# A two-layer decoder step: spilled gates and sums fetched ahead, a round's branch product in two halves around its transposes, and one weight split a step later

## The chip, the cores and the metric

The kernel runs on one core of a Trainium2 chip. TensorE (PE, with its weight loads PEld) multiplies, VectorE (DVE), ScalarE (ACT) and GpSimd (POOL) do the rest, and SyncE (SP) only issues transfers. The metric is the device time of one execution in microseconds (us); lower is better.

## The reference

One inference step of a decoder with two layers, for a prompt of 256 tokens and 64 sample tokens, which the kernel handles as one block of T = 320 columns. What matters here is how a layer ends:

```python
def _layer(x, ...):                       # prompt group: 256 tokens; sample group: 8 x 8 tokens with 2048 cached keys each
    xn = _rmsnorm(x, norm_g)
    h = xn @ w_in                         # one projection: pool, MLA and DeltaNet inputs, z gates, 3 x 1024 branch gates
    y_a = pool_mixer(h_pool) * silu(z_pool)
    y_b = mla(h_q, h_kv, h_kr, cached latents) * silu(z_mla)
    y_c = _rmsnorm(gated_delta(conv(h_qkv), beta, alpha)) * silu(z_dn)
    gates = sigmoid(h_gate)               # (tokens, 3, 1024)
    merged = (gates[:, :, 0] * (y_a @ w_br_pool) + gates[:, :, 1] * (y_b @ w_br_mla)
              + gates[:, :, 2] * (y_c @ w_br_dn))
    return x + merged @ w_out, caches and states
# two layers, then a final RMSNorm
```

## The kernel before

Activations lie transposed, 128 channels on the partitions and 320 tokens along the free dimension. A fp32 product is made of three fp32r products: a weight tile `wraw` comes from DRAM on SP's queue (four buffers), ACT rounds it into a high part `wh` (L200), DVE subtracts to get the low part `wl` (L201), and `mm3` (L224 to L226) issues for each 128-row block k the three matmuls wh by high, wh by low, wl by high. A buffer of `wraw` is free again when its `wl` is made.

Each layer goes through these stages:

1. Projections and DeltaNet. Of the branch gates, those of the DeltaNet branch (n = 1) and of the attention branch (n = 2) are computed along the way, 16 tiles of 128 x 320 (160 KB) a layer, and **spilled** to DRAM (`spilled[n, m]`, m being one of 8 slices of 128 output channels).
2. Prompt attention, one head a step (h = 0 to 10, a software pipeline): PE makes scores `hsc`; DVE takes maxima; ACT takes the exponential (`pS`); DVE takes a reciprocal and POOL scales (`head_scale`); PE transposes (`pT`), ACT copies (`pPT`), PE multiplies by the values (`po`). Two gates are computed in these steps; at h = 5 the weights of the second are split.
3. Eight **rounds**, one for each sample sequence bb. In a round PE makes the pool branch's gate product for slice m = bb (`gate`), a small product `olat` for the round before, eight transposes of the softmaxed scores `S` (`PT`) and one of the own keys (`PTn`), the pool branch's product `br` with w_br_pool (12 matmuls), the attention product `pv`, and the scores `sc` of the next sequence. DVE transposes the next sequence's keys (`flip`); POOL issues the gathers of later keys. At the end DVE forms (gate + 1) times `br` and ACT's queue stores it to DRAM as `sums[m]` (`first_sum`). All of these take banks from one PSUM pool "A" with four banks.
4. The **tail**: 16 branch products, n = 1 and 2 for m = 0 to 7; each goes into a bank, and `branch_out(n, m, b)` fetches the gate tile `gt` on POOL's queue (NG = 6 buffers), for the first product of a slice also `accs[m]` from `sums[m]` (four buffers `acc`), multiplies on DVE (L1360) and adds on POOL (L1361). The finished slice is halved and split by ACT and DVE into `mgH`, `mgL`, and eight products with w_out (24 matmuls each, tile `wo`) follow; each is added to the residual `xT`, which POOL's queue brings back from DRAM (1280 KB) near the start of the tail.

In stages 2 and 3 and at the start of the tail the order of PE, DVE, ACT and POOL is the order in which the code is written; after it a scheduler orders the instructions. Each engine executes in order: an instruction that waits holds up all behind it, and a transfer is issued only when the issuing engine comes to it. The lines around the transposes in a round:

```python
PT = turned_p(S)
PTn = turned_own(bb)
b = branch_mm(0, w0, "A")
weigh(bb, mx)
```

Of the kernel before, what the change touches and what calls it, by code (L numbers as in the profile page):

```python
# [11 lines left out]
F32 = mybir.dt.float32  # L12
# [19 lines left out]
KVB = 3  # L32
WSP = 2
THB = 2
NG = 6
ORD0 = (4, 5)
PRM, RNB, STB, XT, WLP = "M", "M", "M", ("A", "B"), 2
WARM, WN, TA = 8, 6, 1
# [78 lines left out]
def trunk(tc, I, O, layers=2):  # L117
    nc = tc.nc
# [24 lines left out]
    def ps(tag, name):  # L143
        return (banks.get(tag) or banks["pool"]).tile([128, 512], F32, tag=tag, name=name, bufs=banks["n"][tag])
# [269 lines left out]
    for l in range(layers):  # L414
# [931 lines left out]
            wname = branches[n][1]  # L1346
            return split_w(load_w(I[wname][l][:, m * 128 : m * 128 + 128], 4, 128)[:, :4, :], 4)

        def branch_mm(n, w, tag):
            b = ps(tag, "br")  # L1350
            mm3(b[:, :T], w, yb[branches[n][2]], 4)
            return b

        def branch_out(n, m, b):
            t = per.tile([128, T], F32, tag="gt", name="gt", bufs=NG)
            nc.gpsimd.dma_start(t, spilled[n, m])
            if m not in accs:
                accs[m] = p3a.tile([128, T], F32, tag="acc", name="acc", bufs=4)
                nc.gpsimd.dma_start(accs[m], sums[m])
            stt(t, t, 1.0, b[:, :T], add, mult)  # L1360
            nc.gpsimd.tensor_tensor(accs[m], accs[m], t, add)  # L1361

# [9 lines left out]
        with tc.manual_schedule(engines={mybir.EngineType.PE, mybir.EngineType.DVE, mybir.EngineType.Activation, mybir.EngineType.Pool}):  # L1372
# [23 lines left out]
            for h in range(11):  # L1396
                if h < 8:
                    hsc = hp_.tile([128, 512], F32, tag="H", name="hsc", bufs=4)
                    head_scores(h, hsc)
                    st2 = head_max(hsc)  # L1400
                    hs[h] = head_soften(hsc, st2), st2
                if h < 2:
                    values(h)
                if h == 4:
                    gather(1)
                if h == 5:
                    nm, w = gate_w()
                if h in flips:
                    flip(0, keys, flips[h])
                if h - 2 in hs:  # L1410
                    hp[h - 2] = head_turned(hs[h - 2][0])
                if h in (2, 3):
                    b = gate_mm("A", w, b, (4 * (h - 2), 4 * (h - 2) + 4))
                if h in (7, 8):
                    b = gate_mm("A", w, b, (4 * (h - 7), 4 * (h - 7) + 4))
                if h in hs:
                    head_scale(*hs[h])
                if h - 3 in hs:
                    head_attend(h - 3, hp[h - 3])
                if h == 3:  # L1420
                    gate_out(nm, b)
                    b = None
                if h == 8:
                    gate_out(nm, b)
                    pair[0] = paired[0] = 1
                    gs = gate_w(nm=(0, 0)), branch_w(0, 0)
                if h == 9:
                    hpc.close()
                    sp = bank4(spc, "sp")
                    sc = scores(keys, q4)  # L1430
# [6 lines left out]
            for bb in range(NB):  # L1437
                more = bb + 1 < NB
                if not more:

                    pdc.close()
                    p3a = p3e.enter_context(tc.tile_pool(name=f"p3a_{l}", bufs=1, reuse_waits="tile"))
                S = soften(bb, sc, mx)
                if more:
                    keys = key_tiles()
                    flip(bb + 1, keys, 0)
                    nmx = stats(bb + 1)
                softened(bb, S, mx)
                if more:
                    flip(bb + 1, keys, 1)  # L1450
                (nm, w), w0 = gs
                g = gate_mm("A", w)
                if o is not None:
                    ob = combine(o)
                    combined(bb - 1, ob)
                t = gate_out(nm, g)
                if more:
                    flip(bb + 1, keys, 4)
                    flip(bb + 1, keys, 2)
                PT = turned_p(S)  # L1460
                PTn = turned_own(bb)
                b = branch_mm(0, w0, "A")
                weigh(bb, mx)
                if not more:
                    w10 = branch_w(1, 0)
                    split_y(p3a, 8)
                    w11 = branch_w(1, 1)
                o = attend(bb, PT, PTn, mx)
                first_sum(bb, t, b)
                if more:  # L1470
                    flip(bb + 1, keys, 3)
                    gs = gate_w(nm=(0, bb + 1)), branch_w(0, bb + 1)
                    sc = scores(keys, q4)
                    mx = nmx
                    if bb + 2 < NB:
                        q4 = load_q(bb + 2)
# [23 lines left out]
            last = l == layers - 1  # L1500
            p3c, p3 = enter(f"p3_{l}", dict(pj=2, Y=2) if last else dict(pj=4))
            wcfg.update(pool=p3, n=2)
            w13 = branch_w(1, 3)
            split_y(p3, 4)
            w20 = branch_w(2, 0)
# [12 lines left out]
        for mp in range(4):  # L1518
# [3 lines left out]
                        branch(n, m, "A")  # L1522
            for m in (2 * mp, 2 * mp + 1):
                split_x(mg[0][:, m, :], mg[1][:, m, :], accs[m], scale=0.5)
        nm = Norm(p3)
        if last:

# [71 lines left out]
```

## Time and profile before

| | |
|---|---|
| Time, median of 3 runs | 1073.99 us (1073.39 to 1076.58) |
| The profiled execution's own time | 1067.52 us |
| Its span, first to last instruction | 1065.8 us |
| PE busy | 984.4 us (92%) |
| DVE busy | 692.1 us (65%) |
| ACT busy | 474.8 us (45%) |
| POOL busy | 279.2 us (26%) |
| Mean granted TensorE clock | 0.979 of full speed |

Busy time is the time in which an engine had an instruction under way; matmuls overlap, so their durations sum to more than the time they take. The profiled execution is 0.6% below the median of the other three. In a timeline the column after the start is the time from the start of the first to the end of the last of the instructions merged in the row, and the bracket gives the idle time of the engine before it and what ended it. Rows of `DMA_DIRECT2D` or `DMA_INDIRECT` on an engine are the issuing of a transfer, not its landing.

### The profile page before, as it was taken

The page shows a single profiled execution, that of the slowest core. Times are in us where ns is not written, and L with a number is a line of the kernel's source. Part 1 is how long each engine was busy: PE and PEld are TensorE (multiplying, and loading weights), DVE is VectorE, ACT ScalarE, POOL GpSimd, SP SyncE. Part 2 cuts the span into 40 slices and gives each one's busy share as a digit, 9 for nine tenths or more (in the row PEclk, how much of TensorE's full clock was granted, in tenths as well). Part 3 has the DMA queues.
Part 4 walks back from the last instruction along what each step waited for, and adds up shares of the span by engine and source line. Part 5 has one row for each costly group of instructions (what it writes and reads, how often), then busy time and mean ns, then how long its engine had stood idle before and what let it go on. Part 6 is the DMA issues. An engine that isn't in the chain of part 4 may idle for free. (4 is left out here: it accounts for less than half of the span.)

```text
span 1065.8 us, 24832 instructions
## 1 busy us (share of the span) xinstructions
PE 984.4 (92%) x10211; PEld 858.9 (81%) x10211; DVE 692.1 (65%) x1364; ACT 474.8 (45%) x878; POOL 279.2 (26%) x412
## 2 busy tenths in 40 slices
PE   8998999989999999978999999997999999999686
PEld 7897988978877877868888889896878777778686
DVE  4879857557546756555668997744565666575462
ACT  6664353364353323333567544426426433234243
POOL 1224113124242111036313432221241410102441
PEclk9999999999999999999999999998999999999898
DMA  8644444633564676368564454453356366644651
GB/s 231 185 132 112 120 114 109 168 86 97 156 217 149 202 247 224 104 194 248 142 182 130 115 139 112 110 149 84 95 146 193 136 212 218 234 156 149 206 172 50
DMA packets 206538, 165.78 MB, mean 156 GB/s; under 512 B 28344, under 2 KB 195026, under 8 KB 203850
## 3 DMA queue, kind: packets, MB, share of 16 engines
q1 hardware_dynamic: 176364, 98.47, 34.2%
q0 software_dynamic: 8384, 52.03, 13.8%
q10 hardware_dynamic: 21678, 13.71, 4.2%
q8 instruction: 80, 1.31, 0.5%
q14 instruction: 32, 0.26, 0.1%
HBM read 147.45 MB, written 16.96 MB: 154 GB/s over the span
## 5 line engine op out<-in xcount | busy, mean ns | idle before, releaser
L201 DVE TENSOR_TENSOR wl<-wraw,wh 128x1024 fp32r<-128x1024 f32 (+1 forms) x180 | 195.6, 1099 | 116.1 <-ACT wh L200 115.8
L200 ACT ACTIVATE wh<-wraw 128x1024 fp32r<-128x1024 f32 (+1 forms) x180 | 166.0, 936 | 168.8 <-PE pj L225 54.4
L226 PE MATMUL pj<-xnH,wl 128*128 128x320 f32 (+1 forms) x528 | 170.0, 322 | 6.9 <-DVE wl L201 6.8
L224 PE MATMUL pj<-xnH,wh 128*128 128x320 f32 (+1 forms) x528 | 170.6, 323 | 4.7 <-ACT wh L200 1.7
L225 PE MATMUL pj<-xnL,wh 128*128 128x320 f32 (+1 forms) x528 | 167.5, 317 | 0.0
L224 PE MATMUL gate<-xnH,wh 128*128 128x320 f32 x384 | 122.2, 318 | 0.8 <-DVE qn L982 0.6
L226 PE MATMUL gate<-xnH,wl 128*128 128x320 f32 x384 | 120.1, 313 | 0.3 <-DVE wl L201 0.3
L225 PE MATMUL gate<-xnL,wh 128*128 128x320 f32 x384 | 119.3, 311 | 0.1
L226 PEld LDWEIGHTS pj<-xnH,wl 128*128 128x128 f32 (+1 forms) x528 | 101.0, 191 | 11.9 <-DVE wl L201 10.1
L224 PEld LDWEIGHTS pj<-xnH,wh 128*128 128x128 f32 (+1 forms) x528 | 101.0, 191 | 10.8 <-issue 4.9
L225 PEld LDWEIGHTS pj<-xnL,wh 128*128 128x128 f32 (+1 forms) x528 | 101.0, 191 | 1.2
L1195 DVE STREAM_TRANSPOSE KT<-kv 128x1024 f32<-128x1024 f32 x64 | 78.7, 1230 | 0.6
L224 PEld LDWEIGHTS gate<-xnH,wh 128*128 128x128 f32 x384 | 72.2, 188 | 7.6 <-issue 6.5
L224 PE MATMUL br<-yH,wh 128*128 128x320 f32 x192 | 63.8, 332 | 15.0 <-DVE gt L1360 14.9
L226 PEld LDWEIGHTS gate<-xnH,wl 128*128 128x128 f32 x384 | 72.2, 188 | 2.1 <-DVE cy L524 0.8
L225 PEld LDWEIGHTS gate<-xnL,wh 128*128 128x128 f32 x384 | 72.2, 188 | 0.8 <-issue 0.4
L226 PE MATMUL br<-yH,wl 128*128 128x320 f32 x192 | 61.0, 319 | 3.9 <-DVE wl L201 3.9
L225 PE MATMUL br<-yL,wh 128*128 128x320 f32 x192 | 60.9, 317 | 0.0
L1205 PE MATMUL sc<-KT,q 32*64 32x256 f32 x2048 | 59.3, 377 | 0.0
L1276 PE MATMUL pv<-kv,PT 128*64 128x256 f32 x512 | 58.8, 382 | 0.0
L1235 ACT ACTIVATE S<-S,mx 128x1024 f32<-128x1024 f32 x16 | 18.4, 1149 | 84.5 <-DVE mx L1234 72.3
L1205 PEld LDWEIGHTS sc<-KT,q 32*64 32x64 f32 x2048 | 45.8, 131 | 12.0 <-issue 5.7
(410 smaller groups left out, 2016.1 us busy)
## 6 DMA issues: line engine op xcount, KB each, us to landing
wraw<-in_w_in SPq DMA_DIRECT2D x114, 512.0 KB
wraw<-in_w_out SPq DMA_DIRECT2D x16, 512.0 KB
gate<-gt ACTq DMA_DIRECT2D x32, 160.0 KB
gt<-gate POOLq DMA_DIRECT2D x32, 160.0 KB, 3.3
q<-q4d SPq DMA_DIRECT2D x64, 72.0 KB
wraw<-in_w_br_pool SPq DMA_DIRECT2D x16, 256.0 KB
wraw<-in_w_br_dn SPq DMA_DIRECT2D x16, 256.0 KB
wraw<-in_w_br_mla SPq DMA_DIRECT2D x16, 256.0 KB
```

What stands on the lines that cost most here:

```text
L200: act(h, raw, AF.Copy)
L201: (nc.gpsimd.tensor_tensor if spare or turn[0] in K["lo"] else tt)(lo, raw, h.bitcast(F32), sub)
L224: nc.tensor.matmul(out, wh[:, k, :], xh[:, first + k, :], start=k == 0, stop=False)
L225: nc.tensor.matmul(out, wh[:, k, :], xl[:, first + k, :], start=False, stop=False)
L226: nc.tensor.matmul(out, wl[:, k, :], xh[:, first + k, :], start=False, stop=k == nk - 1)
L1195: nc.vector.transpose(v[:, a], kv[:, a * 1024 : a * 1024 + 1024].rearrange("p (i k c) -> p i k c", i=4, k=8))
L1205: nc.tensor.matmul(sc[64 * hf : 64 * hf + 64, g, :256], q4[r, k, :], krT[r, keys_] if k == 8 else KT[r, k, keys_], start=k == 0, stop=k == 8,)
L1235: act(S, S, AF.Exp, bias=mx[:, 4:5], accum_out=mx[:, 5:6])
L1276: nc.tensor.matmul(pv[64 * hf : 64 * hf + 64, :256], PT[:, n * 128 + 64 * hf : n * 128 + 64 * hf + 64], kv[:, r : r + 256], start=n == 0, ...
```

## The change

- **Gates and sums.** `branch_out` no longer fetches. Seven gate tiles (NG is 7 now) are fetched at the start of round 4 into the lasting pool, the first four sums at the start of round 7, and the other nine gate tiles at the start of the tail, one right after the other, into nine buffers of their own (`gt3`). The sums of slices 4 to 7 are fetched when slices 0 to 3 have been split and their buffers are free.
- **Rounds.** The branch product of a round is issued in two halves: k = 0 and 1 ahead of the nine transposes, k = 2 and 3 behind them.
- **Head steps.** At h = 5 the split of the second gate's weights stands behind the transposes' copy and the head's scaling and not ahead of them.

The diff, with the functions that it calls:

```diff
--- before.py
+++ after.py
@@ -32,7 +32,7 @@
 KVB = 3
 WSP = 2
 THB = 2
-NG = 6
+NG = 7
 ORD0 = (4, 5)
 PRM, RNB, STB, XT, WLP = "M", "M", "M", ("A", "B"), 2
 WARM, WN, TA = 8, 6, 1
@@ -1346,17 +1346,28 @@
             wname = branches[n][1]
             return split_w(load_w(I[wname][l][:, m * 128 : m * 128 + 128], 4, 128)[:, :4, :], 4)
 
-        def branch_mm(n, w, tag):
-            b = ps(tag, "br")
-            mm3(b[:, :T], w, yb[branches[n][2]], 4)
+        def branch_mm(n, w, tag, b=None, ks=None):
+            b = b or ps(tag, "br")
+            mm3(b[:, :T], w, yb[branches[n][2]], 4, ks=ks)
             return b
 
+
+        used = [(1, 0), (1, 1), (1, 2), (1, 3), (2, 0), (2, 1), (2, 2), (2, 3)]
+        used += [(n, m) for mp in (2, 3) for n in (1, 2) for m in (2 * mp, 2 * mp + 1)]
+        ready = {}
+
+        def fetch(pool, tag, n):
+            for _ in range(n):
+                nm = used.pop(0)
+                ready[nm] = pool.tile([128, T], F32, tag=tag, name="gt", bufs=n)
+                nc.gpsimd.dma_start(ready[nm], spilled[nm])
+
+        def fetch_sum(m):
+            accs[m] = p3a.tile([128, T], F32, tag="acc", name="acc", bufs=4)
+            nc.gpsimd.dma_start(accs[m], sums[m])
+
         def branch_out(n, m, b):
-            t = per.tile([128, T], F32, tag="gt", name="gt", bufs=NG)
-            nc.gpsimd.dma_start(t, spilled[n, m])
-            if m not in accs:
-                accs[m] = p3a.tile([128, T], F32, tag="acc", name="acc", bufs=4)
-                nc.gpsimd.dma_start(accs[m], sums[m])
+            t = ready[n, m]
             stt(t, t, 1.0, b[:, :T], add, mult)
             nc.gpsimd.tensor_tensor(accs[m], accs[m], t, add)
 
@@ -1403,8 +1414,6 @@
                     values(h)
                 if h == 4:
                     gather(1)
-                if h == 5:
-                    nm, w = gate_w()
                 if h in flips:
                     flip(0, keys, flips[h])
                 if h - 2 in hs:
@@ -1415,6 +1424,8 @@
                     b = gate_mm("A", w, b, (4 * (h - 7), 4 * (h - 7) + 4))
                 if h in hs:
                     head_scale(*hs[h])
+                if h == 5:
+                    nm, w = gate_w()
                 if h - 3 in hs:
                     head_attend(h - 3, hp[h - 3])
                 if h == 3:
@@ -1440,6 +1451,10 @@
 
                     pdc.close()
                     p3a = p3e.enter_context(tc.tile_pool(name=f"p3a_{l}", bufs=1, reuse_waits="tile"))
+                    for m in range(4):
+                        fetch_sum(m)
+                if bb == 4:
+                    fetch(per, "gt", NG)
                 S = soften(bb, sc, mx)
                 if more:
                     keys = key_tiles()
@@ -1457,9 +1472,10 @@
                 if more:
                     flip(bb + 1, keys, 4)
                     flip(bb + 1, keys, 2)
+                b = branch_mm(0, w0, "A", ks=(0, 2))
                 PT = turned_p(S)
                 PTn = turned_own(bb)
-                b = branch_mm(0, w0, "A")
+                branch_mm(0, w0, "A", b, (2, 4))
                 weigh(bb, mx)
                 if not more:
                     w10 = branch_w(1, 0)
@@ -1500,6 +1516,7 @@
             last = l == layers - 1
             p3c, p3 = enter(f"p3_{l}", dict(pj=2, Y=2) if last else dict(pj=4))
             wcfg.update(pool=p3, n=2)
+            fetch(p3, "gt3", 16 - NG)
             w13 = branch_w(1, 3)
             split_y(p3, 4)
             w20 = branch_w(2, 0)
@@ -1522,6 +1539,8 @@
                         branch(n, m, "A")
             for m in (2 * mp, 2 * mp + 1):
                 split_x(mg[0][:, m, :], mg[1][:, m, :], accs[m], scale=0.5)
+                if m < 4:
+                    fetch_sum(m + 4)
         nm = Norm(p3)
         if last:
```

How the order of instructions moves, at three places. First PE, in a round of layer 0, as a piece of the difference (`br` is the branch product's bank, `PT` and `PTn` the transposes):

```order
 L1288 MATMUL olat<-cst,o 128x64 x2
-L1253 MATMUL PT<-cst,S 128x128 x8
-L1262 MATMUL PTn<-cst,so 64x64
 L224 MATMUL br<-yH_3477,wh 128x320
 L225 MATMUL br<-yL_3478,wh 128x320
...
 L225 MATMUL br<-yL_3478,wh 128x320
 L226 MATMUL br<-yH_3477,wl 128x320
+L1253 MATMUL PT<-cst,S 128x128 x8
+L1262 MATMUL PTn<-cst,so 64x64
 L224 MATMUL br<-yH_3477,wh 128x320
 L225 MATMUL br<-yL_3478,wh 128x320
```

Six of the twelve matmuls of the branch product now stand between `olat` and the transposes, six behind them. It is so in all 16 rounds.

Second POOL, from the last round into the tail of layer 0, before the change (`gate_0` and so on are the spilled gates in DRAM, `xs` the residual in DRAM):

```order
L1240 TENSOR_TENSOR mx<-mx 128x1 x2
L1356 DMA gt<-gate_0_221 128x320
L1359 DMA acc<-sum_0_237 128x320
L1361 TENSOR_TENSOR acc<-acc,gt 128x320
L1356 DMA gt<-gate_1_222 128x320
L1359 DMA acc<-sum_1_238 128x320
L1517 DMA xT<-xs_218 128x2560
L1361 TENSOR_TENSOR acc<-acc,gt 128x320
L1356 DMA gt<-gate_4_225 128x320
L1359 DMA acc<-sum_2_239 128x320
L1361 TENSOR_TENSOR acc<-acc,gt 128x320
```

And with the change, from the same place on:

```order
L1240 TENSOR_TENSOR mx<-mx 128x1
L1372 TENSOR_TENSOR acc<-acc,gt 128x320
L1534 DMA xT<-xs_218 128x2560
L1372 TENSOR_TENSOR acc<-acc,gt 128x320
L1363 DMA gt<-gate_7_228 128x320
L1363 DMA gt<-gate_8_229 128x320
...
L1363 DMA gt<-gate_15_236 128x320
L1372 TENSOR_TENSOR acc<-acc,gt 128x320 x6
L1367 DMA acc<-sum_4_241 128x320
```

Before, each fetch of a gate stands behind the addition of the product before it. Now the first seven gates and four sums have been issued earlier, the other nine gates are issued in one go behind the residual, and six additions stand behind that.

Third ACT, in the head steps of layer 0, as a piece of the difference:

```order
 L1317 ACTIVATE pS,st_3774<-hsc,st_3774 128x128
 L1318 ACTIVATE pS,st_3774<-hsc,st_3774 128x256
-L200 ACTIVATE wh<-wraw 128x1024
-L1331 ACTIVATE pPT<-pT 128x384
+L1331 ACTIVATE pPT<-pT 128x384
+L200 ACTIVATE wh<-wraw 128x1024
 L1317 ACTIVATE pS,st_3804<-hsc,st_3804 128x128
```

The copy of the transposes now comes ahead of the weights' rounding; on DVE the reciprocal likewise moves ahead of `wl`.

## Rows read from the trace of the kernel before

**Rows 1.** The page's first part: busy time, share of the span and instructions.
```profile
PE 984.4 (92%) x10211; PEld 858.9 (81%) x10211; DVE 692.1 (65%) x1364; ACT 474.8 (45%) x878; POOL 279.2 (26%) x412
```

**Rows 2.** Waits of PE, whole span: who waited for whom: us in total, times, longest.
```profile
PE br L224 <- DVE gt L1360: 14.9, 8, 2.5
PE PT L1253 <- ACT S L1235: 8.6, 13, 1.4
...
PE br L226 <- DVE wl L201: 3.9, 4, 1.3
...
PE wo L225 <- DVE mgL L210: 2.1, 1, 2.1
...
PE wo L224 <- ACT mgH L209: 1.7, 1, 1.7
PE po L1338 <- ACT pPT L1331: 1.7, 2, 0.8
...
PE pT L1329 <- POOL pS L1324: 1.1, 2, 0.6
```

**Rows 3.** Timeline of PE, layer 0: start, duration, instruction, count, [idle before it <- releaser].
```profile
337.99 1.09 PE L1253 MATMUL PT<-cst,S 128*128 128x128 f32 x8 [1.39 <-ACT S L1235]
...
385.23 0.56 PE L1288 MATMUL olat<-cst,o 128*128 128x64 f32 x4
386.32 1.09 PE L1253 MATMUL PT<-cst,S 128*128 128x128 f32 x8 [0.54 <-ACT S L1235]
```

**Rows 4.** Timeline of ACT and POOL in the round of Rows 3's last row.
```profile
386.75 0.47 ACT L465 ACTIVATE gt<-gt 128x320 f32<-128x320 f32 x1
386.80 0.19 POOL L1240 TENSOR_TENSOR mx<-mx 128x1 f32<-128x1 f32 x1 [8.46 <-ACT so L1236]
387.12 1.07 ACT L1254 ACTIVATE PT<-PT 128x512 f32<-128x512 f32 x2
```

**Rows 5.** Timeline of POOL, then of DVE, at the start of layer 0's tail.
```profile
460.75 1.24 POOL L1361 TENSOR_TENSOR acc<-acc,gt 128x320 f32<-128x320 f32 x1 [8.75 <-DVE gt L1360]
...
463.05 0.54 POOL L1517 DMA_DIRECT2D xT<-xs  x1
466.12 0.95 POOL L1361 TENSOR_TENSOR acc<-acc,gt 128x320 f32<-128x320 f32 x1 [2.53 <-DMA acc<-sum]
467.01 0.56 POOL L1356 DMA_DIRECT2D gt<-gate  x1
...
472.66 1.25 POOL L1361 TENSOR_TENSOR acc<-acc,gt 128x320 f32<-128x320 f32 x1 [4.54 <-DVE gt L1360]
...
472.09 0.49 DVE L1360 SCALAR_TENSOR_TENSOR gt<-gt,br 128x320 f32<-128x320 f32 x1 [2.26 <-DMA gt<-gate]
```

**Rows 6.** Timeline of PE: first and last products of the tails of layers 0 and 1.
```profile
457.53 0.41 PE L224 MATMUL br<-yH,wh 128*128 128x320 f32 x1
...
528.08 0.31 PE L226 MATMUL wo<-mgH,wl 128*128 128x320 f32 x1
...
529.84 0.31 PE L226 MATMUL wo<-mgH,wl 128*128 128x320 f32 x1
...
975.64 0.41 PE L224 MATMUL br<-yH,wh 128*128 128x320 f32 x1
...
1055.26 0.31 PE L226 MATMUL wo<-mgH,wl 128*128 128x320 f32 x1
```

**Rows 7.** One 2 us stretch: busy time per engine (instructions), granted clock, DMA share, GB/s.
```profile
480.00:482.00 2.00, 1.91 (x8) 1.51 (x6) 0.00 (x0) 0.32 (x1) 0.03 (x1) 0.50 0.57 173
```

**Rows 8.** DMA in 980 to 992 us: packets, MB, share of 16 engines; last, KB and us to landing.
```profile
q0 software_dynamic: 336, 1.97, 47.5%
q1 hardware_dynamic: 2110, 1.05, 29.6%
...
xT<-xs POOLq DMA_DIRECT2D x1, 1280.0 KB, 8.2
```

**Rows 9.** Timeline of ACT in the tail of layer 1.
```profile
991.19 1.24 ACT L200 ACTIVATE wh<-wraw 128x512 fp32r<-128x512 f32 x2 [6.78 <-DMA wraw<-in_w_br_mla]
```

## The prediction

> **What bounds the kernel now.** The page's busy times come first: PE is busy 92% of the span, no other engine comes near [rows 1]. So time can only come from PE's idle stretches or from matmuls at the lower clock. PE's waits over the whole span are therefore the second view [rows 2]. The largest entry is the branch product waiting for DVE's multiplication of an older one (14.9 us, 8 times: no PSUM bank is free), the next is the transposes `PT` waiting for the softmaxed scores (8.6 us, 13 times). The change aims at both, and at two small ones of the head steps (1.7 and 1.1 us).
>
> Third, the timelines say who is late behind those names. In the tail DVE's multiplication itself waits 2.26 us for the gate tile [rows 5]. That tile was issued by POOL at 467.01, right behind the addition at 466.12, which had waited 2.53 us for its sum; the next addition starts at 472.66 [rows 5]. So POOL walks a chain of issue, landing and addition that takes 472.66 - 466.12 = 6.5 us a product. PE needs 12 matmuls for one; 12 take 529.84 - 528.08 = 1.76 us [rows 6], 0.147 us each. The chain, not PE, sets the pace of the first products of a tail.
>
> Fourth, how much a tail loses in all. Layer 0's runs from 457.53 to the last `wo` matmul at 529.84, plus 0.15: 72.5 us. Layer 1's runs from 975.64 to 1055.26: 79.8 us [rows 6]. Its 16 x 12 + 8 x 24 = 384 products take 384 x 0.147 = 56.3 us at full clock. Lost: 16.2 and 23.5 us. That is more than the listed waits, for after one of these stalls the clock is low: in 480 to 482 us it is 0.50 granted, which is 1.2 GHz, and PE gets 8 matmuls into 2 us where 13.6 fit [rows 7].
>
> **The change, part by part.**
>
> *Tails.* Seven gates and four sums are there before the tail begins, so the first seven multiplications wait for PE alone, and the chain is gone. What stays out of reach or comes new:
> - The small products `olat` and `oml` between branch products, and in layer 1 the output's transposes: not waste, they stay.
> - Weights. DVE's low parts made PE wait 3.9 us in 4 places [rows 2]; part of it came from DVE standing at a late gate. I keep half, 1 us a layer. Worse is the traffic: residual (1.31 MB) and nine gates (1.47 MB) now go out in one burst of 2.8 MB. In 980 to 992 us, where a residual also landed, POOL's queue moved 1.97 MB and SP's 1.05 MB [rows 8]: 0.164 MB a us, and four 256 KB weights in 12 us, 3 us each; one made ACT wait 6.78 us [rows 9]. At that rate the burst lasts 17 us. In it 5.7 weights arrive and PE could use 17 / 1.76 = 9.7. The four `wraw` buffers and the split tiles behind them are a lead of about four products. So the lack is 0 to 4 products, 0 to 7 us a layer; nearer to 0, since the lead is full when the burst begins. I take 1 us.
> - POOL's additions. Six stand behind nine issues of some 0.55 us [rows 5], and the burst's landing may hold the last of these issues: the residual alone took 8.2 us to land [rows 8]. DVE and ACT come to `mgH`, `mgL` of the first slices only ten products in (18 us), the additions start about 14 us in (463.05 + 8.2 - 457.53). Nothing is lost there; 0 to 4 us (the waits of `wo` were 2.1 and 1.7 us, [rows 2]); I take 0.5.
> In sum I leave 4.5 us of layer 0's loss and 7.5 of layer 1's, and gain 11.7 + 16.0 = 27.7 us.
>
> *Rounds.* In a round PE ends `olat` at 385.23 + 0.56 = 385.79 and idles 0.54 us to 386.32, when `S` is ready [rows 3]. Six matmuls of `br` take 6 x 0.147 = 0.88 us and cover that wholly. In round 0 the wait is 1.39 us [rows 3], of which 0.51 stays. With 13 waits, 2 x 1.39 + 11 x 0.53 = 8.6 as listed; the gain is 8.6 - 2 x 0.51 = 7.6 us. Is it given back at `pv`, which needs ACT's copies of the transposes and now has six matmuls ahead of it and not twelve? The transposes would start at 386.67, 0.35 later, so ACT's copies, which ran from 387.12 to 388.19 behind the tanh of 386.75 [rows 4], end near 388.5. PE, after 1.09 us of transposes, the own keys and 0.88 of `br`, reaches `pv` at 388.64 at the earliest, and `pv` needs the second copy only for its second half: covered, by little. `br` holds its bank longer, but `pv` takes a bank that ACT has emptied, not that of `br`, whose reader on DVE stands behind `pv`. Bounds: 0 to 8.6.
>
> *Fetches ahead.* Seven issues of 0.55 us are 3.9 us on POOL in round 4, four are 2.2 in round 7. Behind them stand the `mx` addition and the gathers of the keys. POOL idled 8.46 us before such an addition [rows 4], so the issues cost nothing; without that cover they would put up to 3.9 us on the next gather, which has a round of lead. I take 0; bound 2 us a layer.
>
> *Head steps.* The copy ahead of the rounding removes the wait of `po` (1.7 in both layers), the reciprocal ahead of `wl` that of `pT` (1.1) [rows 2]. But DVE's `wl` then waits for a rounding that starts later, and the next maxima stand behind it, so the next transposes come late. Bounds -1 to 2.8 us, taken 1.
>
> Sum: 27.7 + 7.6 + 1 = 36.3 us. The profiled execution took 1067.5, so 1031.2 of its kind; it lies 6.5 below the median of the runs, and against that median, 1074.0, the forecast is **1038 us**.
>
> *A rule against it.* In [rows 8] a packet on POOL's queue is 1.97 MB / 336 = 5.9 KB and on SP's 0.5 KB, and in the same stretch SP's queue still got 35% of the bytes. The Trainium skill (DMA: Bandwidth & Descriptors, section "Queues, rings and completion order") says that a transfer engine alternates between queues packet by packet; a queue of small packets would then get 0.5 of 6.4, 8%. By that rule (an estimate from the page and these packets) almost no weight would come in the 17 us, a layer would lose 5.7 products or 10 us, and the sum would be near 1056. The trace does not bear so steep a share out. The first rival is what a milder form of it gives.
>
> **The rivals.**
> - *Weights become the bound* in both tails. For it: 3 us a weight and the 6.78 us wait [rows 8, 9]. Against it: the burst ends, and the four products of lead. If the lead is empty, 7 us a layer, and a stretch at 1.2 GHz behind the stall (some 21 matmuls at twice 0.147: 2.5 us more than else [rows 7]) make 9.5 a layer; 19 less the 2 already taken gives 1055.
> - *POOL becomes late.* Its additions start behind the burst, the sums of slices 4 to 7 behind them, and `wo` waits for `mgH`, `mgL` as in layer 1 now [rows 2]: 4 us and a clock loss of 2 a layer, 12 in all: 1049.
> - *The wait in the round only moves* from `PT` to `pv`, if ACT's copies come 0.5 us later than worked out: the 7.6 us are lost: 1045. For it: ACT must do a tanh first [rows 4].
> - *Slower.* If a weight takes x us not just in the burst but for all 14 that a tail loads, the tail takes 14x plus 33 us (two branch products and the output). It decides at 14x + 33 = 72.5 + 4.3 (half of what rounds and head steps give), x = 3.1. The burst alone shows 3.0; at 4 us throughout, 1074 + 2 x 14 x 0.9 = 1099. Against it: nothing but weights is left to load once the burst is over.
>
> **How the numbers follow.** Forecast 0.60, weights 0.18, POOL 0.10, the moved wait 0.07, slower 0.03, no visible change 0.02. A difference under 0.3% can hardly be told from none here (the runs before span 1073.4 to 1076.6). Faster is 0.60 + 0.18 + 0.10 + 0.07 = 0.95, same 0.02, slower 0.03. The range: if the tails keep only half of what I leave them (6 us more) and rounds and head steps give all (1.0 and 1.8 more), 1029; at the other end the weights' rival, 1055.
>
> **What would show it.** Right: no waits of `br` for the multiplication in L1371; `PT` waits only in round 0; tails near 61 and 64 us; clock 1.0 through the branch products. Wrong: ACT's rounding waiting for `wraw` and PE for `wh` or `wl` in the tails; `pv` waiting for `PT`; POOL's additions late and `wo` waiting for `mgH`; a gather late in round 5 or 6.

## The result and the profile after

The changed kernel takes **1039.83 us** (median of 4 runs, 1039.05 to 1040.8) against 1073.69 (4 runs, 1070.58 to 1076.58): the ratio is 0.9686, with a 95% interval of 0.9657 to 0.9714. The forecast was 1038, its range 1029 to 1055. The profiled execution took 1039.05 us with a span of 1037.2.

First the page's busy times and PE's waits over the whole span, as in [rows 1, 2]:

```profile
PE 980.9 (95%) x10211; PEld 858.6 (83%) x10211; DVE 691.3 (67%) x1364; ACT 476.5 (46%) x878; POOL 287.6 (28%) x412
```

```profile
PE wo L225 <- DVE mgL L210: 1.9, 3, 1.0
PE br L226 <- DVE wl L201: 1.9, 4, 0.6
...
PE br L224 <- ACT wh L200: 1.7, 2, 1.0
PE wo L224 <- ACT mgH L209: 1.6, 2, 0.9
...
PE PT L1253 <- ACT S L1235: 1.0, 2, 0.5
```

The largest entry of before, the branch product behind DVE's multiplication (14.9 us), is gone. The transposes wait twice and not 13 times. The largest new entry is `br` waiting for ACT's rounded weights `wh`; the other new ones are 0.8 us or less. The granted clock is 1.00 through the branch products, in 454 to 494 and in 958 to 990 us; the kernel before has 0.91 in 470 to 490.

PE's timeline of a round (compare the last two rows of [rows 3]); the first row is round 0, the others are round 2 of layer 0:

```profile
339.71 1.09 PE L1253 MATMUL PT<-cst,S 128*128 128x128 f32 x8 [0.50 <-ACT S L1235]
...
369.27 0.56 PE L1288 MATMUL olat<-cst,o 128*128 128x64 f32 x4
369.63 0.39 PE L224 MATMUL br<-yH,wh 128*128 128x320 f32 x1
...
370.60 1.03 PE L1253 MATMUL PT<-cst,S 128*128 128x128 f32 x8
```

PE's timeline at both ends of the tails (compare [rows 6]):

```profile
454.24 0.41 PE L224 MATMUL br<-yH,wh 128*128 128x320 f32 x1
...
517.64 0.31 PE L226 MATMUL wo<-mgH,wl 128*128 128x320 f32 x1
...
958.89 0.41 PE L224 MATMUL br<-yH,wh 128*128 128x320 f32 x1
...
1026.65 0.31 PE L226 MATMUL wo<-mgH,wl 128*128 128x320 f32 x1
```

With 0.15 us for the last start they are 63.6 and 67.9 us long; they were 72.5 and 79.8. POOL's timeline at the start of layer 0's tail (compare [rows 5]), and the row of ACT that stands out there:

```profile
457.46 1.25 POOL L1372 TENSOR_TENSOR acc<-acc,gt 128x320 f32<-128x320 f32 x1 [10.22 <-DVE gt L1371]
458.66 0.56 POOL L1534 DMA_DIRECT2D xT<-xs  x1
460.74 1.25 POOL L1372 TENSOR_TENSOR acc<-acc,gt 128x320 f32<-128x320 f32 x1 [1.51 <-DVE gt L1371]
461.94 3.76 POOL L1363 DMA_DIRECT2D gt<-gate  x7
467.28 1.08 POOL L1363 DMA_DIRECT2D gt<-gate  x2 [1.59 <-DMA xT<-xs]
468.38 2.51 POOL L1372 TENSOR_TENSOR acc<-acc,gt 128x320 f32<-128x320 f32 x3
```

```profile
469.73 0.63 ACT L200 ACTIVATE wh<-wraw 128x512 fp32r<-128x512 f32 x1 [6.71 <-DMA wraw<-in_w_br_mla]
```

The first additions now wait for products and no longer for transfers. But the nine issues and the residual form the burst of which the prediction spoke: its last two issues waited 1.59 us for the residual's landing, and ACT stood 6.71 us without a weight.

**The stages.** The end of a tail and the start of the next stage can be read from the same timeline in every kernel: the first head score `hsc`, the first `br` behind a layer's last `pv`, the last `wo`. The table holds the differences, in us, for all runs told of below (numbers of two layers as a / b); the stages are those of the one profiled execution of each kernel, the time is the median of all:

| Kernel | time, median | start to first hsc | head steps and rounds | tail | sum of tails | layer 0's tail to layer 1's hsc |
|---|---|---|---|---|---|---|
| before | 1073.7 | 299.5 | 158.0 / 157.7 | 72.5 / 79.8 | 152.2 | 287.9 |
| before again (e4) | 1068.9 (one) | 302.6 | 158.0 / 157.7 | 74.2 / 78.4 | 152.6 | 286.0 |
| e1 fetches only | 1052.9 | 303.9 | 158.2 / 157.7 | 63.7 / 67.2 | 130.9 | 291.6 |
| e2 halves only | 1061.0 | 302.3 | 152.9 / 153.1 | 74.7 / 80.2 | 154.9 | 289.6 |
| e3 weights later only | 1069.1 | 302.3 | 157.1 / 157.0 | 72.3 / 79.5 | 151.8 | 288.8 |
| changed kernel | 1039.8 | 301.9 | 152.3 / 152.5 | 63.6 / 67.9 | 131.5 | 288.6 |
| changed again (e9) | 1037.6 | 301.3 | 152.4 / 153.0 | 62.7 / 70.3 | 132.9 | 290.3 |
| e5 residual late | 1047.9 | 303.5 | 152.5 / 152.2 | 64.6 / 72.1 | 136.8 | 287.2 |
| e6 eight sums ahead | 1035.9 | 299.1 | 152.5 / 152.8 | 60.9 / 67.3 | 128.2 | 287.8 |
| e7 no burst | 1037.1 | 304.6 | 152.6 / 152.4 | 60.3 / 65.0 | 125.3 | 291.0 |
| e8 nine and three | 1037.3 | 304.5 | 152.2 / 151.8 | 63.6 / 66.3 | 129.9 | 289.0 |
| e10 no burst, nine and three | 1034.8 | 302.5 | 152.0 / 151.6 | 61.2 / 66.7 | 127.9 | 287.2 |
| e11 as e10, eight sums | 1033.4 | 301.3 | 152.6 / 151.7 | 61.3 / 63.6 | 124.9 | 288.5 |
| e12 sums late | 1053.6 | 302.7 | 152.1 / 152.1 | 65.4 / 71.7 | 137.1 | 297.5 |

One execution of e12 took 3214 us and is left out of its median.

What no edit touches (the third and the last column) varies by 5 to 6 us between executions. In e1 and e12 the last column holds something else too: by their traces the scheduler put this stretch in another order, while in all others the order of PE, DVE, ACT and POOL there is the same but for two instructions at most. The tails differ with their order as well. It is one and the same in the kernel before, e4, e2 and e3 (sums of tails 151.8 to 154.9), in the changed kernel, e9, e8 and e1 (129.9 to 132.9), and in e7 and e10 (125.3 and 127.9). So a sum of tails varies by some 3 us with nothing changed in it. Stage lengths still say more of an edit than one total does. In the medians of three later sets of runs the kernel before took 1071.6 (17 runs), 1072.5 (7) and 1071.4 (11).

### The profile page after: what moved, and what is told of

Read it like the earlier page. It is cut to its first block, busy times and chain, and to the rows that moved or that the text cites. A ratio compares the mean times of both kernels' runs of the same rounds, so it can differ in the third digit from the quotient of the medians.

```text
span 1037.2 us, 24844 instructions
## 1 busy us (share of the span) xinstructions
PE 980.9 (95%) x10211; PEld 858.6 (83%) x10211; DVE 691.3 (67%) x1364; ACT 476.5 (46%) x878; POOL 287.6 (28%) x412
## 4 chain that ended last, share of the span: by engine, by line
PE 62%; DVE 15%; ACT 7%; DMA 6%; issue 6%; POOL 2%; ACTq 1%; SPq 0%; DVEq 0%; POOLq 0%
PE sc L1205 6%; PE pv L1276 6%; PE pj L224 5%; PE pj L226 5%; PE pj L225 4%; DVE wl L201 4%; PE gate L224 4%; PE gate L225 3%; PE gate L226 3%; DVE cy L524 3%; DMA wraw<-in_w_out 2%; PE wo L225 2%; PE br L224 1%; PE wo L226 1%; ACT wh L200 1%
## 5 line engine op out<-in xcount | busy, mean ns | idle before, releaser
L201 DVE TENSOR_TENSOR wl<-wraw,wh 128x1024 fp32r<-128x1024 f32 (+1 forms) x180 | 198.1, 1110 | 101.9 <-ACT wh L200 101.3
L225 PEld LDWEIGHTS gate<-xnL,wh 128*128 128x128 f32 x384 | 72.3, 188 | 0.5
```

Of the source, the lines that this page charges most:

```text
L201: (nc.gpsimd.tensor_tensor if spare or turn[0] in K["lo"] else tt)(lo, raw, h.bitcast(F32), sub)
L225: nc.tensor.matmul(out, wh[:, k, :], xl[:, first + k, :], start=False, stop=False)
```

## The experiments

**e1 to e3: each part alone.** The edits are the hunks of the change, one group at a time. e1 keeps `fetch`, `fetch_sum` and NG = 7; e2 and e3 are:

```diff
-                PT = turned_p(S)
-                PTn = turned_own(bb)
-                b = branch_mm(0, w0, "A")
+                b = branch_mm(0, w0, "A", ks=(0, 2))
+                PT = turned_p(S)
+                PTn = turned_own(bb)
+                branch_mm(0, w0, "A", b, (2, 4))
```

```diff
-                if h == 5:
-                    nm, w = gate_w()
                 if h in flips:
...
                     head_scale(*hs[h])
+                if h == 5:
+                    nm, w = gate_w()
```

> The kernel before with the gates and sums fetched ahead (seven gates at round 4, four sums at round 7, nine gates in one burst at the tail's start), and neither the halves of the branch product nor the moved weights. Theory: the tails' gain is that of the fetches alone. The changed kernel's tails are 63.6 and 67.9 us long (72.5 and 79.8 before, 20.8 us less), so here they should be the same within 1 us each, the rounds should be as in the kernel before (16.1 us from one row of transposes to the next, a wait of PT in each), and the time 1050 us (1046 to 1054). Rival: the tails gain in part because the rounds before them run otherwise (weights that come earlier, another phase of the transfers); then the tails here are longer than 66 and 70 us and the time is 1055 or more.

> The kernel before with nothing but the branch product of a round in two halves around its transposes. Theory: each round loses its wait of PT (0.53 us) and a little more, some 5 us a layer, as the changed kernel's 15.4 us from one row of transposes to the next (16.1 before) say: 1064 us (1061 to 1067), tails as in the kernel before. Rival: the halves gain only together with the other parts (the wait moves to pv, or the tail starts earlier and waits the longer for its gates): 1070 or more, with waits of pv, or tails longer than 74 and 81 us.

> The kernel before with nothing but the second head gate's weights split one place later at h = 5. Theory: the waits of po (1.7 us in both layers) and of pT (1.1) shrink or go, a wait of the gate product for zs and of later transposes comes for them; 1 us less over both layers, which the times can hardly tell: 1073 us (1070 to 1076), the stretch from the first hsc to the first PT shorter by 0.3 to 1.3 us a layer. Rival: the maxima that now stand behind the later subtraction make the head steps longer: 1 to 3 us more in that stretch.

Measured: 1052.86 us (1048.5 to 1054.6, ratio 0.9816, interval 0.9791 to 0.9841), 1060.98 (1054.8 to 1064.8; 0.9893, 0.9864 to 0.9921) and 1069.14 (1065.5 to 1076.2; 0.9982, 0.996 to 1.0005), against 1071.62 for the kernel before on the same chip. The theory holds for e1 and e2 (e2's tails aside), both rivals fall. e1's tails are the changed kernel's (63.7 / 67.2), its rounds those of before; e2's rounds are the changed kernel's and its tails, in the same order, are 2.7 us longer in sum than before. From the first `hsc` to the first `PT` e3 takes 37.75 and 37.65 us where the kernel before takes 38.48 and 38.37 us: 0.7 us a layer less. e3's whole time can't be told from none. By the medians the parts add: 18.8 + 10.6 + 2.5 = 31.9 us below 1071.6, and the changed kernel's median lies 31.8 below it. So close a fit is luck, since e3's 2.5 can't be told from nothing.

**e4: the kernel before, once more.** No edit.

> The kernel before, unchanged, profiled once more: its profiled execution was 6 us below the median of its runs. Theory: the executions differ in the tails, where POOL's chain of issue, landing and addition depends on how long each transfer takes; the stages ahead of the tails agree within 2 us, and a slower execution has longer tails than 72.5 and 79.8 us. Rival: they differ in the stages ahead (start, projections, DeltaNet), and the tails agree within 1 us.

One execution, 1068.93 us. The theory falls: one tail is 1.7 us longer and the other 1.4 shorter, the sums agree within 0.4 us, while the start is 3.0 us later and the stretch between the layers 2.0 shorter. The rival holds for the start; that each tail agrees within 1 us does not. Executions differ in both places.

**e5 and e6: parts of the burst moved.** e5 holds the residual back behind the sixth addition; e6 brings the last four sums forward into the burst.

```diff
-        nc.gpsimd.dma_start(xT, xs[l])
+        with tc.issue_after(added.ins):        # added: the addition of product (2, 1)
+            nc.gpsimd.dma_start(xT, xs[l])
```

```diff
-            accs[m] = p3a.tile([128, T], F32, tag="acc", name="acc", bufs=4)
+            accs[m] = p3a.tile([128, T], F32, tag="acc", name="acc", bufs=8)
...
             fetch(p3, "gt3", 16 - NG)
+            for m in range(4, 8):
+                fetch_sum(m)
...
-                if m < 4:
-                    fetch_sum(m + 4)
```

> The changed kernel with the residual xT fetched behind the sixth addition of the tail and not ahead of the second. Theory: what is left of the tails' loss comes in good part from the burst (residual 1.31 MB and nine gates 1.47 MB at once), which keeps weights off: ACT's rounding waited 6.7 us for a weight in layer 0 and PE 2.0 us for wh and wl in layer 0, 1.5 in layer 1. Without the residual the burst is half as long, these waits go, and the tails are 61 to 62.5 and 65.5 to 67 us (63.6 and 67.9 now): 1036 to 1038 us. Rival: the residual then comes together with the w_out weights (4 MB) and the sums of slices 4 to 7 and keeps those off; the waits move to mgH, mgL and the wl of w_out, and the tails are as long or up to 3 us longer: 1040 to 1045.

> The changed kernel with eight buffers for sums and the sums of slices 4 to 7 fetched right behind the nine gates. Theory: the last additions are late because the sums of slices 4 to 7 are issued only after the splits of slices 0 to 3 and then land among the w_out weights (POOL waits 1.4 us for one in layer 0, 2.2 and 0.7 in layer 1); PE's waits for mgH and mgL (1.7 and 1.9 us), and in layer 1 the low clock behind them (0.75 and 0.82 granted over 8 us), come from that. Ahead of need they cost nothing: tails 61.5 and 64 us, 1034 us (1032 to 1037). Rival: the burst becomes 4 us longer, weights come later still, and the tails gain nothing: 1039 to 1043, with longer waits for wh and wl.

e5: 1047.88 us (1044.7 to 1048.0). The rival came true, and more of it. ACT's timeline (first row) and POOL's in layer 0's tail:

```profile
487.11 0.63 ACT L200 ACTIVATE wh<-wraw 128x512 fp32r<-128x512 f32 x1 [5.83 <-DMA wraw<-in_w_br_mla]
...
489.16 0.54 POOL L1367 DMA_DIRECT2D acc<-sum  x1 [4.24 <-DVE mgL L210]
489.71 11.20 POOL L1372 TENSOR_TENSOR acc<-acc,gt 128x320 f32<-128x320 f32 x8
```

ACT waited 5.83 us for a branch weight whose issue ended at 478.61; the residual, issued at 477.62, landed at 486.03. The split of slice 3 stood behind that weight on ACT, the issue of the last sum (which needs that slice's buffer) behind the split, and all eight last additions behind the issue. One late transfer has stopped ACT, DVE and POOL in turn.

e6: 1035.87 us (1032.5 to 1039.5). Both halves of its expectation show. Layer 0's tail has no wait for `mgH` or `mgL` left and is 60.9 us long; but the longer burst makes PE wait more for `wl`, in layer 0 (first row) and layer 1:

```profile
PE br L226 <- DVE wl L201: 2.1, 2, 1.5
...
PE wo L225 <- DVE mgL L210: 2.5, 1, 2.5
PE br L226 <- DVE wl L201: 1.9, 2, 1.3
```

**e7: no burst.** The lead of seven gates and four sums stays; the other nine gates are fetched one at a time into the seven buffers.

```diff
-            t = ready[n, m]
+            t = ready.get((n, m))
+            if t is None:
+                t = per.tile([128, T], F32, tag="gt", name="gt", bufs=NG)
+                nc.gpsimd.dma_start(t, spilled[n, m])
...
-            fetch(p3, "gt3", 16 - NG)
```

> The changed kernel without the burst of nine: seven gates and four sums come ahead as before, the other nine gates one at a time into the seven buffers as these come free. Theory: the tails lost their time in the first products, whose chain ran without a lead; a lead of seven is enough, and no burst keeps weights off: tails 62 to 64 and 66 to 68 us, 1036 to 1040. Rival: all gates must be ahead; with buffers that come free only when POOL has added, the chain of issue, landing and addition comes back, DVE waits for gt again, and the tails are 66 and 71 us or more: 1046 or more.

1037.07 us (1034.6 to 1038.7), with tails of 60.3 and 65.0 us: better than the theory had it, and 6.2 us shorter in sum than the changed kernel's (7.7 than in its second profile). PE's waits in layer 0's tail are all here:

```profile
PE br L226 <- DVE wl L201: 0.6, 1, 0.6
PE wo L225 <- DVE mgL L210: 0.3, 1, 0.3
PE wo L226 <- DVE wl L201: 0.3, 1, 0.3
```

In the changed kernel the same view of the same tail has `wl` 1.1, `wh` 1.0, `mgL` 1.0 and `mgH` 0.7. POOL's additions and fetches alternate, and no fetch waits for a landing:

```profile
460.35 1.25 POOL L1375 TENSOR_TENSOR acc<-acc,gt 128x320 f32<-128x320 f32 x1 [10.23 <-DVE gt L1374]
461.90 0.56 POOL L1373 DMA_DIRECT2D gt<-gate  x1 [0.30 <-POOL acc L1375]
462.46 0.55 POOL L1536 DMA_DIRECT2D xT<-xs  x1
463.63 1.25 POOL L1375 TENSOR_TENSOR acc<-acc,gt 128x320 f32<-128x320 f32 x1 [0.62 <-DVE gt L1374]
465.18 0.56 POOL L1373 DMA_DIRECT2D gt<-gate  x1 [0.30 <-POOL acc L1375]
```

So the gain of the tails comes from the lead over the first products, and the kernel with the burst of nine has the longer tails. The medians (1037.07 and 1039.83) lie too close to show it, since this kernel's other stages were long in its profile (304.6 and 291.0); e10's tails bear it out (127.9 in sum). Whether the traffic alone does it is not shown: without the burst the scheduler also orders the tail otherwise (ACT's first splits come ahead of some weights, and so on), and no run holds that order fixed.

**e8: nine matmuls ahead of the transposes, three behind.**

```diff
-                b = branch_mm(0, w0, "A", ks=(0, 2))
+                b = branch_mm(0, w0, "A", ks=(0, 3))
...
-                branch_mm(0, w0, "A", b, (2, 4))
+                branch_mm(0, w0, "A", b, (3, 4))
```

> The changed kernel with nine matmuls of the round's branch product ahead of the transposes and three behind (six and six now). Theory: 0.44 us more cover ahead of the transposes takes the rest of round 0's wait of PT (0.50 us, worth 0.66 with the lost overlap) and nothing else: 1.2 us less over both layers, 1038.6. Rival: what stands between the transposes and pv falls from 0.88 to 0.44 us, less than ACT needs for its copies, so pv waits up to 0.44 us (0.6 with the lost overlap) in all 16 rounds, and the kernel is up to 9 us longer: 1045 to 1049, rounds of 16.0 us and waits of pv.

1037.27 us (1036.2 to 1039.5). Round 0's transposes have no listed wait, and `pv` has none either. ACT's copies and the start of `pv` (PE) in round 2 of layer 0:

```profile
374.02 1.09 ACT L1254 ACTIVATE PT<-PT 128x512 f32<-128x512 f32 x2 [0.54 <-PE PT L1253]
...
374.86 0.31 PE L226 MATMUL br<-yH,wl 128*128 128x320 f32 x1
375.10 1.08 PE L1276 MATMUL pv<-kv,PT 128*64 128x256 f32 x8
```

`pv` begins 0.24 us behind the last `br`, as in the changed kernel, though the second copy ends only at 374.02 + 1.09 = 375.11. The margin that the prediction called covered by little is there even with 0.44 us less of it. The rival falls. Head steps and rounds are 0.1 and 0.7 us shorter than in the changed kernel; 0.6 a layer was expected.

**e9 to e11: the changed kernel again, and two that join what helped.** e10 is e7 with e8's halves. e11 is e10 with eight buffers for sums; their last four fetches then need no split slice and are issued in round 7.

> The changed kernel, unchanged, timed and profiled once more beside the two that follow, since executions differ by some 3 us in the stages that no edit touches (first hsc at 299 to 304 us). Theory: head steps and rounds take 152.3 to 152.6 us a layer and the tails 63.6 and 67.9 us within 1.5 us each, and the time is 1037 to 1041 us. Rival: the tails differ as much between executions as between the kernels compared (more than 3 us in their sum of 131.5); then the gain of the kernel without the burst (125.3) isn't shown by its one profile.

> The changed kernel without the burst of nine gates (one at a time behind a lead of seven) and with nine matmuls of a round's branch product ahead of the transposes. Theory: both gains add: tails of 60.3 and 65.0 us (6.2 less than in the changed kernel), round 0's wait of PT gone (1.2 less), so 7 us below the changed kernel on the same chip: 1032 us (1030 to 1036). Rival: the profile of the kernel without the burst was a lucky one, or its gain goes into waits of the next stage: tails over 129 us in sum, a time within 2 us of the changed kernel's.

> As the kernel before this one in the list (no burst, nine and three), and with eight buffers for sums, the sums of slices 4 to 7 too fetched in round 7. Theory: what is left in its tails is the wait for the last merged slices (mgH and mgL, 0.3 us in layer 0 and 1.4 in layer 1, with POOL waiting 2.6 us for a sum that lands among the w_out weights); it goes: tails of 59.5 and 63 us, 1030 us (1028 to 1034). Rival: the sum of slice 7 is stored at the end of round 7, so its fetch holds up POOL ahead of the first addition and the issues behind it; the first additions and fetches start 2 to 4 us later, and the tails are no shorter or longer than 60.3 and 65.0.

On one chip: 1037.58 us (1036.8 to 1042.1), 1034.84 (1029.9 to 1037.0) and 1033.40 (1028.9 to 1035.7); the ratios to the kernel before are 0.9690 (0.9662 to 0.9717), 0.9654 (0.9622 to 0.9685) and 0.9646 (0.9618 to 0.9675). **By the medians e11 is the fastest kernel here, 4.2 us below the changed one**; the intervals of the ratios overlap. The sums of the tails don't, where the same sums are fetched ahead: 131.5, 132.9 (e9), 129.9 (e8) and 130.9 (e1) with the burst, 125.3 (e7) and 127.9 (e10) without. With eight sums they are 128.2 (e6) with it and 124.9 (e11) without. The means with four sums, 131.3 and 126.6, differ by 4.7 us, 2.3 a layer. e9's tails differ from the changed kernel's by 0.9 and 2.3 us, the second more than the 1.5 that its theory allows, so a difference of 2 us in one tail is not evidence. For e10 7 us below the changed kernel were expected; it is 2.7 below, and its tails are 2.6 us longer than those of e7. e11's rival is visible, but cheap. POOL's timeline in layer 0:

```profile
456.92 0.56 POOL L1367 DMA_DIRECT2D acc<-sum  x1 [10.14 <-DMA sum<-gt]
457.50 0.89 POOL L1375 TENSOR_TENSOR acc<-acc,gt 128x320 f32<-128x320 f32 x1
```

The last sum is held until round 7 has stored it. The first addition begins 3.7 us after the tail does (453.80); in e10 it is 3.2 us (454.51 to 457.72).

**e12: gates ahead, sums late.** As e7, but no sum comes ahead; each is fetched at its slice's first addition.

```diff
         def branch_out(n, m, b):
+            if m not in accs:
+                fetch_sum(m)
...
-                    for m in range(4):
-                        fetch_sum(m)
...
-                if m < 4:
-                    fetch_sum(m + 4)
```

> The changed kernel without the burst, and with no sum ahead: each sum is fetched when the first product of its slice is added, as in the kernel before; seven gates come ahead. Theory: POOL's chain has two links, the gate that DVE needs and the sum that the addition needs; DVE's reading, which frees PE's bank, needs the gate alone, so the gates carry the gain of the first products, and the sums only decide when a buffer of gt comes free and when slices are ready: tails 2 to 5 us longer in sum than the 125.3 without the burst, 1037 to 1041 us. Rival: the sums carry as much as the gates (POOL waited 2.53 us for a sum): tails 10 us longer or more, 1045 or more, with DVE waiting for gt again.

1053.57 us (1048.4 to 1054.0). The tails are 137.1 us in sum, 11.8 longer than e7's. That is the rival's size, though not its mark, since DVE doesn't wait for a gate. POOL's timeline:

```profile
463.48 0.54 POOL L1375 DMA_DIRECT2D gt<-gate  x1
469.43 0.86 POOL L1377 TENSOR_TENSOR acc<-acc,gt 128x320 f32<-128x320 f32 x1 [5.40 <-DMA acc<-sum]
...
487.11 1.81 POOL L1377 TENSOR_TENSOR acc<-acc,gt 128x320 f32<-128x320 f32 x2 [3.41 <-DMA acc<-sum]
```

The sum issued at 462.92, next to the residual, landed 6.4 us later, and the additions and issues behind it shift. Of the 26.9 us of tail between the kernel before and e7, gates ahead alone give 15.1 and sums ahead 11.8 more; sums ahead alone were not tried. The time also holds something else: from layer 0's tail to layer 1's `hsc` 297.5 us pass, at least 5.9 more than in all others, with a granted clock of 0.80 in 620 to 645 us. This is the stretch that the scheduler ordered otherwise: some 900 of PE's 2672 instructions stand in another place than in e7. What in that order costs the time was not tried.

## Why the prediction was right, and what was off

The mechanism was right in each part and the result lies 1.8 us from the forecast. Two terms were mis-sized and one reference was off, and the errors partly cancel: that the number came out so close is in part luck.

- **Tails, forecast -27.7 us, measured -20.7** (152.2 to 131.5; -21.3 with the fetches alone). That POOL's chain, not PE, set the pace of the first products is shown: no wait for the multiplication is left. The step that was too small is the loss that stays, above all the waits of weights and of POOL's additions. The prediction left 4.5 and 7.5 us in the two tails but priced only 2.5 of each (1 for low parts, 1 for weights in the burst, 0.5 for POOL); the rest, 2 and 5, was for small products and the output's transposes, which take 1.5 and 3.0. From start to start in the changed kernel's trace, both tails hold 113.6 us of branch and w_out products, 4.5 of those small ones, 8.1 of listed waits of PE, and 5.3 of overlap lost around the waits and of low clock behind them. The last two are 13.4 us against 5.0 priced (33.7 in the kernel before).
- **The burst is one part of this.** 3.0 us over both layers were taken for it, within bounds of 0 to 7 and 0 to 4 a layer; the kernels without it have 4.7 us less in their tails (126.6 for 131.3, their order changed too). Without it the tails are 60.3 and 65.0 in e7 and 61.2 and 66.7 in e10, about what the prediction said with it (near 61 and 64). So waits that have nothing to do with the burst were priced too low as well: 7.3 and 9.9 us are left in e7 and e10, where 2.0 were taken.
- **Where the burst costs.** Its traffic was foreseen well (5.7 weights in 17 us; the queues' rows for 458 to 474 us in the changed kernel show 1.57 MB or 6 weights in 16). The lead of four products was not all there: PE waited for `wh` and `wl` 2.1 us in layer 0's tail and 1.5 in layer 1's. In the four kernels with the burst (this one, e9, e8, e1) these waits of `br` are 2.3 to 3.6 us in all, in e7 and e10 1.2. And a second price had been put at 0.5: additions and splits behind it are late, so `wo` waits for `mgH` and `mgL` 3.5 us in all (4.8 to 6.1 in e9, e8 and e1), where it is 1.7 in e7 and 2.9 in e10. In layer 1 the clock falls behind such a wait; the windows there (busy times of PE, PEld, DVE, ACT, POOL, then the granted clock, DMA share, GB/s):

```profile
994.00:998.00 4.00, 3.01 (x12) 2.75 (x13) 3.11 (x5) 2.83 (x4) 4.00 (x4) 0.75 0.85 231
998.00:1002.00 4.00, 3.02 (x16) 2.76 (x16) 3.44 (x5) 0.94 (x2) 2.29 (x2) 0.82 0.69 195
```

A mean of 0.75 is 1.2 GHz in half of the stretch: 12 and 16 matmuls where 27 fit (part of it the waits themselves).

- **Rounds, forecast -7.6, measured -9.8** (e2: 5.2 and 4.6). The wait was right, and round 0 keeps 0.50 of the 0.51 us foreseen. What the step left out: a listed wait of 0.53 us costs 0.69. A round takes 16.11 us with it and 15.42 without. The wait is counted from the end of `olat` (0.56 us long), but without it the next matmul starts 0.36 us after `olat` does, 0.20 before it ends, about the 0.16 that are missing. Each wait removed here gives that overlap back as well.
- **Head steps, forecast -1, measured -1.4** (e3), from the two waits named; the new one, of the gate product for `zs`, is 0.35 us a layer.
- **Fetches ahead, forecast 0:** the interval from round 4's transposes to round 5's is 15.41 to 16.37 us in the kernels that fetch ahead in halves, on average some 0.3 above the others, against some 0.1 without the fetches: 0.2 us a layer. The cover held.
- **The reference.** The steps as measured give -31.5 (20.7 + 9.8 + 1.4 - 0.4), not -36.3. From 1073.99 that would be 1042.5. The measured 1039.8 is 2.7 below that. The median shown before the forecast was itself 2.0 us above that of the 35 runs taken since (1072.0), which covers most of it.
- **Rivals.** Weights as the bound: in kind yes, in size a quarter (2.3 us a layer for all that goes with the burst, where the rival has 9.5 in place of 1). The rival's 21 matmuls at 1.2 GHz stand in no row, and at twice 0.147 us they would cost 3.1 us and not 2.5; in layer 1 of the changed kernel 13 in a row start 0.27 us apart. POOL late: part of the same price. The wait moved to `pv`: no, not with 0.44 us less cover either (e8). Slower: a weight took 16 / 6 = 2.7 us even in the burst, below the 3.1 at which it decides. A rule of packet by packet between queues (the Trainium skill, DMA: Bandwidth & Descriptors, section "Queues, rings and completion order") would by the prediction's estimate have kept nearly all weights off. The queues' rows in 458 to 474 us of the changed kernel (packets, MB, share of 16 engines; q0 is POOL's, q1 SP's):

```profile
q0 software_dynamic: 576, 2.79, 50.7%
q1 hardware_dynamic: 3162, 1.57, 33.5%
```

By these rows POOL's packets are 4.8 KB and SP's 0.5 KB, and SP's queue got 36% of the bytes, not the 9% of equal turns. The trace does not agree with the rule, if a packet of the profile is what the Trainium skill calls a packet; no run here shows whether it is.

## What to carry to other kernels

When an engine issues, waits and adds in turn, give it a lead that covers the first stall, and stop there: seven gates and four sums ahead gave the gain, and the kernels that fetch nine more in one burst have tails 2.3 us a layer longer and wait more for weights from another queue. Price a wait of TensorE, one removed or one that stays, as the listed idle time plus the overlap of the matmuls on both sides, and add the low clock where a trace shows it behind the wait. Where totals vary by more than the effect, compare the lengths of stages between instructions that all versions share, and see first whether the scheduler left their order alone.

## What had not been expected of the hardware

DVE's subtraction of a w_out weight (128x1024, two inputs in SBUF) takes 1.15 to 1.23 us in all traces where POOL adds nothing beside it, but can take much longer where POOL adds at the same time. DVE's and then POOL's timeline of e7, layer 0:

```profile
485.83 2.88 DVE L201 TENSOR_TENSOR wl<-wraw,wh 128x1024 fp32r<-128x1024 f32 x1 [0.80 <-ACT wh L200]
...
489.03 1.21 DVE L201 TENSOR_TENSOR wl<-wraw,wh 128x1024 fp32r<-128x1024 f32 x1
...
485.90 1.72 POOL L1375 TENSOR_TENSOR acc<-acc,gt 128x320 f32<-128x320 f32 x2
```

2.88 is 1.21 and nearly the whole of POOL's two additions (1.72): the two engines went one after the other. It can be the addition that is late: in the changed kernel a subtraction from 493.33 took 1.21 us, and the addition from 493.56 1.73 us, where one alone takes 0.9. The Trainium skill (SBUF — State Buffer, section "SBUF: two separate sides") says that such an operation of VectorE and one of GpSimd take a shared pair of ports in turns, each for a whole instruction; the rows above agree.
